# An encoder layer on one core: first-phase buffers, order and weight splits rearranged

## The chip, the cores and the metric

One core of a Trainium2 chip runs the whole layer in one launch. The metric is the device time of a launch in microseconds. The core has a tensor engine (PE), a vector engine (VectorE, DVE), a scalar engine (ScalarE, ACT) and a general one (GpSimd, POOL), each with its own instruction queue worked through in order, and DMA engines. SyncE (SP) issues nearly all transfers, ScalarE's queue some small ones.

## The reference

One post-norm layer on 512 tokens of width 1024, all in fp32:

```
h    = layer_norm(x)
proj = h @ w_in                      # 384 q latent | 256 kv latent | 32 rope key | 512 a | 512 g
attention, 8 heads: q = rms_norm(q latent) @ w_qb, k and v = rms_norm(kv latent) @ w_kvb,
                    rotary on 32 of 96 dimensions, softmax, p @ v
conv: a * sigmoid(g) -> depthwise convolution, width 31 -> layer_norm -> silu
h1   = layer_norm(2**0.25 * h + concat(attention, conv) @ w_o)
moe: router softmax, each of 16 experts takes its top 64 tokens,
     down(silu(x @ w_gate) * (x @ w_up)) * gate, added back
out  = layer_norm(2**0.25 * h1 + moe)
```

The expert weights are 16 x 3 matrices of 1024 x 2048 (or 2048 x 1024), some 400 MB; everything else is about 15 MB.

## The kernel before

The program has two phases. The first, up to line 998, does everything ahead of the experts; the second streams the expert weights through a ring of buffers and does each expert's three products (L1199, L1276). SBUF is cut into 20 numbered slots of 8 KB a partition, which serve one purpose after another: a slot that a stage has finished with takes the next weights, and finally the first expert weights (`stream`). So the end of a stage's use sets when later transfers can start.

Products of the first phase are made exact in parts. `split` (L226) copies a weight or activation rounded to fp32r on ScalarE ("hi") and subtracts it on another engine ("lo"); `mm3` (L256) then does three matmuls, hi x hi, hi x lo and lo x hi, at L258, L259 and L260. A projection of 128 columns (`project`) is 8 x 3 of them on 512 tokens.

The order on each engine is worked out by a planner that simulates the program: it takes operations by their place in the text when their inputs are ready in its model. `pin` (L206) keeps chosen operations of an engine in written order, for the engines in the set `ordered`. `filler` gives the convolution taps a place behind everything else.

The stages that the change touches, in order:

- `x` is normalised in four tiles (`xhat`, on ScalarE for even and VectorE for odd tiles), turned on PE (L392) and written as `hT`, hi on ScalarE (L393) and lo on VectorE (L395, L396), for 8 chunks. VectorE and GpSimd are pinned here, ScalarE isn't. The first two groups of w_in are split at the same time: four pieces ahead of the loop, the rest behind it.
- `w_in` comes in seven groups (`load_win`, L304), raw into slots 14 and 15 in turn, split into four pairs of slots (`split_win`).
- `conv_w` and `positions` are loaded by ScalarE's queue into buffers of `tmp()`, a rotation of four (L409 to L414); conv_w is turned by four transposes (L418).
- `glu(j)` projects a and g, does the tanh (L435), gates (L436), and then the 31 taps of the convolution: `n_act` of them on ScalarE (L444, L447), added on GpSimd (L445), the rest on VectorE (L453). It is called with 0, 0, 4 and 4.
- `keys`, `queries` and the values: `heads` projects into a PSUM bank and splits it (hi on ScalarE, lo on VectorE). PSUM has 3 banks of kind "pj", 2 "tr", 1 "st", 1 "cn", 1 "cv". For both pairs of heads in flight, rope keys and zeros are copied first (`copy_to`, L625, L627).
- attention in 16 units (`units`): scores two units ahead, softmax, turns (L757), p @ v (L772). `at(n)` puts side work behind unit n: loads of w_o at 9, splits of its first half at 11 and 13, loads of its second half at 13.
- `output(half, t, n)` multiplies by w_o: the attention half first, then the convolution half, whose norm has been done meanwhile.

## Time and profile before

| | us |
|---|---|
| three runs | 1202.52, 1203.52, 1205.8 |
| median | 1203.52 |
| the profiled execution | 1208.29 |
| its span | 1206.3 |

| engine | busy us | share of the span |
|---|---|---|
| PE, matmuls | 1119.5 | 93% |
| VectorE | 400.4 | 33% |
| ScalarE | 249.6 | 21% |
| GpSimd | 203.2 | 17% |

The span is one execution seen by the hardware profiler; the time around it is what the launch adds. Rows name an engine, the line of the kernel, the operation and `out<-in` by the program's names. An idle time in brackets is put down to the releaser that came last. A line can be that of a helper: L227 and L228 are every `split`. In the stretches each engine has its busy time and its count of instructions, and behind them stand PE's granted clock (1.00 is full), the DMA engines' mean share and GB/s.

### The profile page before, as it was taken

What the parts mean: (1) busy time and instruction counts of PE and PEld (TensorE: products, weight loads), DVE (VectorE), ACT (ScalarE), POOL (GpSimd) and SP (SyncE); (2) the same over time, 40 slices, a digit from 0 to 9 for tenths busy, and PEclk for the clock granted to TensorE, in tenths of its full rate; (3) what the DMA queues carried; (4) which work ended last, traced back from release to release, by engine and by line L of the source; (5) the groups of instructions that cost most, each with busy time, mean ns of one, the idle gap of its engine ahead of it and who ended that gap; (6) DMA issues with size and microseconds to landing.
All of it is one profiled execution on the core that took longest, in us unless ns stands there. A gap on an engine that the chain in (4) does not pass through costs nothing.

```text
span 1206.3 us, 13663 instructions
## 1 busy us (share of the span) xinstructions
PE 1119.5 (93%) x5573; PEld 545.0 (45%) x5573; DVE 400.4 (33%) x905; ACT 249.6 (21%) x448; POOL 203.2 (17%) x234
## 2 busy tenths in 40 slices
PE   5899998999999998999999999999998998899996
PEld 3687776785334343433343334334332433243432
DVE  6799898543011115122021112011210122011252
ACT  4546677321111111101010011001000101010120
POOL 6778467210000007000000000000000000000041
PEclk9899899999999999999999999999999999999999
DMA  6421014777999998999999999999999999999996
GB/s 200 135 84 36 6 71 144 271 268 281 420 429 428 428 393 343 427 430 427 426 427 428 428 426 430 427 426 429 426 428 429 426 428 426 429 426 427 428 427 253
DMA packets 43681, 422.85 MB, mean 351 GB/s; under 512 B 5178, under 2 KB 13187, under 8 KB 18018
## 3 DMA queue, kind: packets, MB, share of 16 engines
q1 hardware_dynamic: 42032, 421.28, 84.3%
q8 instruction: 44, 0.72, 0.2%
q10 hardware_dynamic: 1506, 0.43, 0.2%
q0 software_dynamic: 80, 0.26, 0.1%
q14 instruction: 19, 0.16, 0.0%
HBM read 419.60 MB, written 2.36 MB: 350 GB/s over the span
## 4 chain that ended last, share of the span: by engine, by line
PE 73%; DMA 16%; DVE 6%; ACT 2%; issue 1%; POOL 1%; POOLq 0%; SPq 0%; ACTq 0%; DVEq 0%
PE gu L1199 30%; PE py L1276 16%; DMA b<-in_w_up_dram 6%; PE sg L1044 5%; DMA b<-in_w_down_dram 4%; PE pj L258 4%; PE pj L259 3%; PE pj L260 3%; DMA b<-in_w_gate_dram 3%; PE sg L1091 3%; PE st L772 1%; DVE sq L1210 1%; PE tr L1066 1%; DVE cv L453 1%; DMA s<-in_w_in_dram 1%
## 5 line engine op out<-in xcount | busy, mean ns | idle before, releaser
L1199 PE MATMUL gu<-b,xg 128*64 128x512 f32 x1920 | 439.1, 598 | 22.1 <-DVE sq L1210 10.9
L1199 PEld LDWEIGHTS gu<-b,xg 128*64 128x64 f32 x1920 | 133.8, 137 | 291.1 <-issue 244.5
L1276 PE MATMUL py<-b,sq 128*64 128x512 f32 x976 | 224.1, 598 | 0.0
L1056 POOL COPY sq<-oh 128x256 f32<-128x256 f32 x16 | 5.9, 400 | 799.4 <-PE sg L1250 799.4
L1210 DVE TENSOR_TENSOR sq<-sq,gu 128x512 f32<-128x512 f32 x30 | 20.6, 687 | 292.6 <-PE gu L1199 276.8
L1276 PEld LDWEIGHTS py<-b,sq 128*64 128x64 f32 x976 | 67.3, 136 | 109.4 <-issue 102.2
L258 PE MATMUL pj<-s,s 128*128 128x512 f32 x189 | 78.4, 424 | 7.6 <-ACT q L435 3.2
L1044 PE MATMUL sg<-oh,h 128*128 128x128 f32 x512 | 72.6, 290 | 8.3 <-DVE oh L1035 6.9
L1045 ACT ACTIVATE xg<-sg,gbp 128x128 f32<-128x128 f32 x64 | 29.3, 457 | 237.6 <-PE sg L1044 145.9
L1044 PEld LDWEIGHTS sg<-oh,h 128*128 128x128 f32 x512 | 64.6, 198 | 29.6 <-issue 21.6
L259 PE MATMUL pj<-s,s 128*128 128x512 f32 x189 | 77.1, 408 | 0.0
L228 POOL TENSOR_TENSOR s<-s,s 128x512 fp32r<-128x512 f32 (+2 forms) x54 | 64.8, 1223 | 19.0 <-ACT s L227 12.2
L240 DVE SCALAR_TENSOR_TENSOR mask<-tr,aff,ones_b 128x128 bf16<-128x128 f32 x84 | 26.1, 348 | 120.7 <-PE tr L238 120.7
L260 PE MATMUL pj<-s,s 128*128 128x512 f32 x157 | 63.2, 406 | 0.0
L453 DVE SCALAR_TENSOR_TENSOR cv<-s,q,cv 128x512 f32<-128x512 f32 x83 | 62.2, 749 | 1.7
L1212 ACT ACTIVATE sq<-gu 128x1024 f32<-128x1024 f32 x16 | 16.4, 1024 | 217.9 <-PE gu L1199 217.9
L1095 DVE TENSOR_TENSOR b<-sg,b 128x512 f32<-128x512 f32 x56 | 37.0, 687 | 58.3 <-PE sg L1091 58.3
L1091 PE MATMUL sg<-q,q 128*128 128x512 f32 (+1 forms) x128 | 42.2, 437 | 7.0 <-DVE b L1095 5.9
L1080 ACT ACTIVATE q<-py,gates 64x512 fp32r<-64x512 f32 x30 | 20.5, 682 | 131.7 <-PE py L1276 119.0
L258 PEld LDWEIGHTS pj<-s,s 128*128 128x128 f32 x189 | 37.5, 200 | 16.8 <-ACT q L435 3.7
L1081 DVE SCALAR_TENSOR_TENSOR q<-py,gates,q 64x512 fp32r<-64x512 f32 x30 | 22.5, 748 | 65.2 <-ACT q L1080 65.0
L259 PEld LDWEIGHTS pj<-s,s 128*128 128x128 f32 x189 | 37.4, 198 | 7.1
(288 smaller groups left out, 1112.8 us busy)
## 6 DMA issues: line engine op xcount, KB each, us to landing
b<-in_w_down_dram SPq DMA_DIRECT2D x60, 2048.0 KB, 25.8
b<-in_w_gate_dram SPq DMA_DIRECT2D x60, 2048.0 KB, 27.5
b<-in_w_up_dram SPq DMA_DIRECT2D x60, 2048.0 KB, 28.0
s<-in_w_gate_dram SPq DMA_DIRECT2D x8, 1024.0 KB, 6.8
s<-in_w_in_dram SPq DMA_DIRECT2D x12, 512.0 KB, 5.2
s<-in_w_up_dram SPq DMA_DIRECT2D x6, 1024.0 KB, 7.1
s<-in_w_down_dram SPq DMA_DIRECT2D x6, 1024.0 KB, 11.6
s<-in_w_o_dram SPq DMA_DIRECT2D x4, 1024.0 KB, 7.1
```

The source lines that it names most:

```text
L228: pin(eng, eng.tensor_tensor(lo, src, hi.bitcast(F32), op=OP.subtract))
L258: tensor(nc.tensor.matmul(p, a[0], b[0], start=start, stop=False, **kw))
L259: tensor(nc.tensor.matmul(p, a[0], b[1], start=False, stop=False, **kw))
L260: tensor(nc.tensor.matmul(p, a[1], b[0], start=False, stop=stop, **kw))
L453: nc.vector.scalar_tensor_tensor(part if k < CW - 1 else cva[j], src[k], w[k], cva[j] if k == n_act else part, op0=OP.mult, op1=OP.add)
L1044: nc.tensor.matmul(here, rows, oh[:, t, :], start=t == 0, stop=t == TT - 1)
L1045: nc.scalar.activation(xg[:, cc, :], here, AF.Identity, scale=gbp[:, 0, cc:cc + 1], bias=gbp[:, 1, cc:cc + 1])
L1091: nc.tensor.matmul(pp[h], g[h][rs, ts], parts[h][k][rs, :], start=k == 0, stop=k == 1)
L1095: nc.vector.tensor_tensor(a, pp[h], a, op=OP.add)
L1199: nc.tensor.matmul(p[g * 64:(g + 1) * 64, b, :], xg[:, c, s * CAP:(s + 1) * CAP], ws[a][2 * b + g], start=c == 0, stop=c == DC - 1)
L1210: nc.vector.tensor_tensor(hh[:, x], sg[:, x], p[:, x], op=OP.mult)
L1276: nc.tensor.matmul(py[x * 64:(x + 1) * 64, :], hT2[:, b, j, g * 64:(g + 1) * 64], w[2 * a + hf], start=f == 0 and not last, stop=f == 15)
```

## The change

- `load_win` places groups 2 and 3 in slots 0 and 1 instead of 14 and 15.
- `idle` moves up, takes a kind of bank, and puts 30 matmuls of the identity, whose results nobody reads, ahead of everything on PE.
- ScalarE is pinned from `xhat(2)` on; one piece of a split stands ahead of the `hT` loop, the others one behind each chunk.
- `conv_w` and `positions` are loaded into quarters of slot 18 (`lat`), which the rope tables use later.
- `glu(0)` and `glu(1)` do three taps on ScalarE and GpSimd; `glu(3)` writes its tanh into `kraw[0]`. `load(5)` stands ahead of `glu(1)`.
- Rope keys and zeros of the second pair of heads are copied after the values; `keys(0)` and `queries(0)` use the "tr" banks.
- `split_wo` becomes a generator that goes column half by column half; two pieces are taken behind each of units 11 to 14, and the second half of w_o is loaded behind unit 15.

```diff
@@ -298,7 +298,7 @@
         def load_win(g):
             name, c0, n = WIN_GROUPS[g]
-            raw = slot(14 + g % 2)[:, :8 * n].rearrange("p (c n) -> p c n", c=8)
+            raw = slot((14, 15, 0, 1, 14, 15, 14)[g])[:, :8 * n].rearrange("p (c n) -> p c n", c=8)
             src = w_in[0, :, c0:c0 + n].rearrange("(c p) n -> p c n", p=128)
             raws[g] = raw
             return [lambda a=a: nc.sync.dma_start(raw[:, 4 * a:4 * a + 4], src[:, 4 * a:4 * a + 4]) for a in range(2)]
@@ -356,6 +356,14 @@
                 for _ in g:
                     pass
+        def idle(n, kind="pj"):
+            p = bank(kind)
+            for _ in range(n):
+                tensor(nc.tensor.matmul(p[:, :128], ident, ident, start=True, stop=True))
+        idle(30, "cv")
         hhi = quarters(slot(2, F32R)) + quarters(slot(3, F32R))
         hlo = quarters(slot(4, F32R)) + quarters(slot(5, F32R))
@@ -382,10 +390,10 @@
             vector(nc.vector.bn_aggr(mv[:, 0:2], st))
             pin(G, nc.gpsimd.tensor_scalar(mv[:, 2:3], mv[:, 1:2], LN_EPS, None, op0=OP.add))
             pin(G, nc.gpsimd.tensor_tensor(mv[:, 2:3], mv[:, 2:3], half_n, op=OP.pow))
+        ordered.add(nc.scalar)
         xhat(2)
         xhat(3)
-        for sp in (sp0, sp1, sp0, sp1):
-            next(sp)
+        next(sp0)
         for c in range(DC):
             p = bank("tr")
             for t in range(TT):
@@ -394,6 +402,8 @@
             hf = tmp()
             vector(nc.vector.tensor_scalar(hf, p, vc("eg", c), vc("eb", c), op0=OP.mult, op1=OP.add))
             vector(nc.vector.tensor_tensor(hlo[c], hf, hhi[c].bitcast(F32), op=OP.subtract))
+            next((sp1, sp0)[c % 2], None)
         run(sp0, sp1)
         ordered.clear()
@@ -406,11 +416,11 @@
         load_rows((("qg", q_norm_g, 3), ("kg", kv_norm_g, 2), ("cb", conv_b, 4), ("cg", conv_ln_g, 4),
                    ("cbb", conv_ln_b, 4)))
-        cwrow = tmp()[:CW]
+        cwrow = lat[2][:CW]
         nc.scalar.dma_start(cwrow, conv_w[0])
         rr = tp.tile([128, 2], F32, name="rr")
         nc.scalar.dma_start(rr, rope_rows)
-        pos_i = tmp().bitcast(I32)
+        pos_i = lat[3].bitcast(I32)
         nc.scalar.dma_start(pos_i, bcast(positions, S))
         to_columns(16, 33)
         pw = bank("cn")
@@ -427,11 +437,11 @@
             nc.gpsimd.memset(hp[j][:, 0:CW // 2], 0.0)
             nc.gpsimd.memset(hp[j][:, HP - CW // 2:HP], 0.0)
-        def glu(j, n_act=0):
+        def glu(j, n_act=0, sg=None):
             pa = project(QR + KVR + ROPE + j * 128)
             pg = project(QR + KVR + ROPE + CC + j * 128)
-            sg = tmp()
+            sg = tmp() if sg is None else sg
             nc.scalar.activation(sg, pg, AF.Tanh, scale=0.5)
             nc.vector.scalar_tensor_tensor(hp[j][:, CW // 2:CW // 2 + S], sg, 1.0, pa, op0=OP.add, op1=OP.mult)
             src = [hp[j][:, k:k + S] for k in range(CW)]
@@ -524,13 +534,13 @@
         load(2)
         load(3)
-        glu(0)
+        glu(0, 3)
         rope_tables()
         run(split_win(2))
         load(4)
-        glu(1)
+        load(5)
+        glu(1, 3)
         run(split_win(3))
-        load(5)
         s0, s1, s17 = slot(0, F32R), slot(1, F32R), slot(17, F32R)
         cqn = list(zip(quarters(s0)[:3], quarters(s1)[:3]))
         ckvn = list(zip((quarters(s0)[3], quarters(s1)[3]), quarters(s17)[:2]))
@@ -607,7 +617,7 @@
         rotary(0)
         rotary(1)
-        glu(3, 4)
+        glu(3, 4, kraw[0])
@@ -626,11 +636,14 @@
             else:
                 nc.scalar.activation(dst, src, AF.Identity)
-        for qe, ke, qo, ko in qk:
+        def same_rows(qe, ke, qo, ko):
             for k in range(2):
                 copy_to(k, ke[k][64:96], kpe[k][64:96].bitcast(F32), 64)
                 copy_to(k, ko[k][0:64], kpe[k][0:64].bitcast(F32), 0)
                 copy_to(0, qo[k][0:32], zero[:32].to_broadcast([32, S]), 0)
+        same_rows(*qk[0])
         def heads(i, w, n, src, even, odd, kind):
             p = bank(kind)
             for c in range(n):
@@ -649,14 +662,15 @@
                 for k in range(2):
                     copy_to(k, dst[k], qr[i // 2][32 * n:32 * n + 32, k, :].bitcast(F32), 32 * n)
-        keys(0, "pj")
-        queries(0, "pj")
+        keys(0, "tr")
+        queries(0, "tr")
         vt = quarters(slot(14))
         for i in range(4):
             p = bank()
             for c in range(2):
                 mm3(p, tuple(z[:, i * 128:(i + 1) * 128] for z in ckvn[c]), wv[c], c == 0, c == 1)
             nc.scalar.activation(vt[i], p, AF.Identity)
+        same_rows(*qk[1])
         wo, raw_wo = {}, {}
@@ -673,14 +687,17 @@
         def split_wo(half, q, raw, pair, engines):
             hi, lo = (slot(i, F32R).rearrange("p (c n) -> p c n", c=2) for i in pair)
-            for c in range(2):
-                for a in range(2):
+            for a in range(2):
+                for c in range(2):
                     cs = slice(a * 512, (a + 1) * 512)
                     split(hi[:, c, cs], lo[:, c, cs], raw[:, c, cs], engines[2 * c + a])
-            for c in range(2):
-                for n in range(2):
-                    i = (2 * q + c, n) if half == 0 else (4 + 2 * c + n, q)
-                    wo[i] = tuple(z[:, c, n * 512:(n + 1) * 512] for z in (hi, lo))
+                    i = (2 * q + c, a) if half == 0 else (4 + 2 * c + a, q)
+                    wo[i] = tuple(z[:, c, cs] for z in (hi, lo))
+                    yield
+        def pieces(n):
+            for i in range(n):
+                next(wo_split[i % 2], None)
         vrows.append(tp.tile([32, 128], F32, name="vrow0"))
@@ -818,13 +835,17 @@
                 split(cg_hi[j], cg_lo[j], sf, nc.gpsimd)
                 grp.append((cg_hi[j], cg_lo[j]))
+        wo_split = []
         def at(n):
             if n == 9:
                 raw_wo[0] = load_wo(0, 0, 15), load_wo(0, 1, 6)
-            if n == 11:
-                split_wo(0, 0, raw_wo[0][0], (12, 13), (G, G, V, G))
-            if n == 13:
-                split_wo(0, 1, raw_wo[0][1], (0, 1), (V, G, V, G))
+            if n == 10:
+                wo_split.extend((split_wo(0, 0, raw_wo[0][0], (12, 13), (G, G, V, G)),
+                                 split_wo(0, 1, raw_wo[0][1], (0, 1), (V, G, V, G))))
+            if 10 < n < 15:
+                pieces(2)
+            if n == 15:
                 raw_wo[1] = load_wo(1, 0, 6), load_wo(1, 1, 15)
             if 1 <= n < 9:
                 residual((n - 1) // 2, (n - 1) % 2)
@@ -877,9 +898,9 @@
         pm = conv_mean()
         for n in range(2):
             take(output(0, 2, n))
-        split_wo(1, 0, raw_wo[1][0], (2, 3), (G, G, V, V))
+        run(split_wo(1, 0, raw_wo[1][0], (2, 3), (G, G, V, V)))
         pvv = conv_norm(pm)
-        split_wo(1, 1, raw_wo[1][1], (4, 5), (G, G, G, V))
+        run(split_wo(1, 1, raw_wo[1][1], (4, 5), (G, G, G, V)))
         for n in range(2):
             take(output(0, 3, n))
         conv_out(pvv)
@@ -942,12 +963,6 @@
         def end_ranks(t):
             for e in range(2):
                 count(t, first_counts(e), masks.pop((t, e)))
-        def idle(n):
-            p = bank()
-            for _ in range(n):
-                tensor(nc.tensor.matmul(p[:, :128], ident, ident, start=True, stop=True))
         order = [(t, n) for n in range(2) for t in range(TT)]
         ordered.add(nc.tensor)
```

## Rows read from the trace of the kernel before

**Rows 1.** The page: busy us and share; DMA issues, KB each, us to landing

```profile
PE 1119.5 (93%) x5573; PEld 545.0 (45%) x5573; DVE 400.4 (33%) x905; ACT 249.6 (21%) x448; POOL 203.2 (17%) x234
...
s<-in_w_o_dram SPq DMA_DIRECT2D x4, 1024.0 KB, 7.1
```

**Rows 2.** Waits of PE, 0 to 290 us: total, times, longest, us

```profile
PE tr L392 <- ACT h L372: 7.7, 2, 4.1
PE cn L418 <- DMA q<-in_conv_w_dram: 3.9, 1, 3.9
PE pj L258 <- ACT q L435: 3.2, 2, 2.6
PE pj L258 <- DVE s L228: 2.5, 1, 2.5
```

**Rows 3.** Stretches of the first phase: length, busy us (instructions) per engine

```profile
31.94:46.33 14.39, 9.85 (x36) 7.72 (x36) 8.48 (x14) 4.69 (x9) 9.97 (x13) 0.76 0.57 172
46.33:113.54 67.21, 67.21 (x297) 55.25 (x297) 64.80 (x91) 34.91 (x63) 49.55 (x48) 1.00 0.21 65
113.54:130.75 17.21, 12.12 (x33) 9.32 (x34) 15.77 (x23) 9.50 (x17) 13.72 (x12) 0.70 0.11 31
130.75:180.00 49.25, 48.77 (x304) 36.73 (x303) 45.58 (x78) 37.79 (x81) 26.99 (x41) 1.00 0.12 43
180.00:195.50 15.50, 12.80 (x67) 7.88 (x65) 14.02 (x24) 11.81 (x26) 12.28 (x14) 0.89 0.38 134
```

**Rows 4.** The same view, ten-microsecond stretches of the expert phase

```profile
280.00:290.00 10.00, 10.00 (x57) 4.54 (x57) 1.53 (x10) 1.37 (x3) 0.00 (x0) 1.00 0.19 52
470.00:480.00 10.00, 10.00 (x46) 3.19 (x44) 5.70 (x4) 1.02 (x1) 7.89 (x6) 0.92 0.72 280
490.00:500.00 10.00, 10.00 (x56) 4.71 (x55) 1.05 (x3) 1.03 (x3) 0.00 (x0) 1.00 1.01 434
```

**Rows 5.** Chain that ended last, 0 to 130 us: start, us, what

```profile
29.69 6.10 DMA q<-in_conv_w_dram
38.90 0.43 PE pj L259
```

**Rows 6.** ScalarE in order of time, 11 to 33 us: start, us, [idle before]

```profile
11.67 0.63 ACT L227 ACTIVATE s<-s 128x512 fp32r<-128x512 f32 x1 [2.46 <-DMA s<-in_w_in_dram]
13.32 1.24 ACT L372 ACTIVATE h<-h,mve 128x1024 f32<-128x1024 f32 x1 [0.50 <-DMA s<-in_w_in_dram]
31.59 0.76 ACT L393 ACTIVATE s<-tr,q 128x512 fp32r<-128x512 f32 x1
```

**Rows 7.** Waits of SP's queue, 0 to 320 us

```profile
SPq L304 <- POOL s L228: 27.3, 8, 8.9
```

**Rows 8.** PE in order of time, one run of filler matmuls

```profile
271.71 1.95 PE L950 MATMUL pj<-ident 128*128 128x128 f32 x16
```

**Rows 9.** Groups by line, 0 to 290 us: busy, mean ns | idle before

```profile
L228 POOL TENSOR_TENSOR s<-s,s 128x512 fp32r<-128x512 f32 (+2 forms) x54 | 64.8, 1223 | 19.0 <-ACT s L227 12.2 <-PE pj L259 5.3 <-DMA q<-in_w_router_dram 1.5
...
L453 DVE SCALAR_TENSOR_TENSOR cv<-s,q,cv 128x512 f32<-128x512 f32 x83 | 62.2, 749 | 1.7
...
L445 POOL TENSOR_TENSOR s<-s,q 128x512 f32<-128x512 f32 x6 | 8.1, 1355 | 1.8 <-ACT q L444 1.8
```

**Rows 10.** VectorE in order of time, the last convolution tap

```profile
197.19 0.74 DVE L453 SCALAR_TENSOR_TENSOR s<-hp,q,cv 128x512 f32<-128x512 f32 x1
```

**Rows 11.** ScalarE in order of time, 114 to 116 us

```profile
114.43 1.13 ACT L627 ACTIVATE s<-s 64x512 fp32r<-64x512 f32 x2
115.47 0.57 ACT L435 ACTIVATE q<-pj 128x512 f32<-128x512 f32 x1
```

**Rows 12.** ScalarE in order of time, at 181 us

```profile
181.74 1.15 ACT L227 ACTIVATE s<-s 128x512 fp32r<-128x512 f32 x2 [1.09 <-DMA s<-in_w_o_dram]
```

**Rows 13.** SP's queue in order of time, the second w_o half

```profile
188.55 2.38 SPq L670 DMA_DIRECT2D s<-in_w_o_dram  x2
```

**Rows 14.** PE in order of time, first use of the conv group's low part

```profile
236.51 0.39 PE L260 MATMUL pj<-s,sq 128*128 128x512 f32 x1
```

## The prediction

> **What bounds the kernel now.** The page comes first: TensorE is busy for 93% of the span [rows 1], so the time can fall only where TensorE idles or runs at its lower clock. Next, the waits of PE up to 290 us (the first phase) show where it idles: 3.9 us in front of the four conv_w transposes, 2.6 us behind a tanh (L435), 2.5 us behind a subtraction on VectorE (L228), and a stall of 4.1 us before any projection [rows 2]. The stretches of that phase add the clock, the third number from the end of a row (one level is 2.4 GHz, 1.00, the other 1.2): 0.76, 0.70 and 0.89 in the three stretches with those stalls and a later one, 1.00 in the two between, where PE is busy nearly all the time [rows 3]. So I read each bad stretch as useful work (busy time times granted clock) and loss. From 31.94 to 46.33 us that is 9.85 x 0.76 = 7.5 us of work in 14.4, a loss of 6.9. From 113.54 to 130.75 it is 12.12 x 0.70 = 8.5 in 17.2, a loss of 8.7. From 180 to 195.5 it is 12.80 x 0.89 = 11.4 in 15.5, a loss of 4.1 [rows 3]. Together 19.7 us.
>
> Does a gain there reach the end? In the expert phase DMA moves 434 GB/s at 490 us, but 52 GB/s at 280 us and 280 GB/s at 470 us while PE is busy all through both stretches [rows 4]: up to 480 us the weight stream waits for PE to free buffers, and after it the stream sets the pace. Both start from PE's progress, so what PE gains before 280 us I carry to the end one for one.
>
> **The change part by part.**
>
> *conv_w and positions into `lat`.* The transposes of conv_w stand in PE's queue before further projection matmuls. Their transfer is issued only at 29.69 us, when a `tmp()` buffer is free, and takes 6.10 us [rows 5]. In `lat[2]`, unused until the rope tables, it can be issued in the first microseconds. The stall of 3.9 us goes and so does the half clock behind it, where a matmul takes 0.43 us [rows 5] against 67.21 / 297 = 0.23 [rows 3]. Of the 6.9 us I leave about 0.6 for the tanh wait at the stretch's end (L435 has 3.2 us in two waits, the longest 2.6 [rows 2]): 6.3 us. Bounds 0 and 6.9. What is late next there is hT: the last ScalarE writes of it come at 31.59 us and after, behind splits of later w_in groups [rows 6]; the next edit is for that.
>
> *ScalarE pinned, splits interleaved.* At present ScalarE waits 2.46 us for w_in, does a split at 11.67 and reaches the third normalised tile only at 13.32 [rows 6]. In written order that tile goes first: 0 to 13.32 - 11.67 = 1.65 us earlier. The fourth tile, on VectorE, must come too, so I take half, 0.8 us. Eight splits between eight hT writes cost nothing that PE sees: ScalarE is busy 4.7 of 14.4 us there [rows 3]. GpSimd's subtractions keep the same order with them.
>
> *w_in groups 2 and 3 into slots 0 and 1, load(5) earlier.* SP's queue waits 27.3 us in eight waits for splits to free slots 14 and 15 [rows 7]. Four transfers no longer do, and conv_w travels on ScalarE's queue, not behind them. PE has no wait on w_in in [rows 2], so this is worth nothing by itself; it keeps the later groups from being late when the projections start earlier, and without it part of those 27.3 us would come to stand on PE's path.
>
> *30 filler matmuls at the start.* Sixteen such take 1.95 us [rows 8], so 30 take about 3.7, or 7.3 at half clock, while PE has nothing else. Worth 0 to 2.4 us: the upper end is the half-clock part of the conv_w loss, 6.9 - 3.9 - 0.6. I take 0, since stalls of up to 4.1 us lie between the fillers and the first projection [rows 2], and stalls of 2.6 and 2.5 us were enough to leave a stretch at 0.70 [rows 2, 3]. The Trainium skill ("TensorE: Matmul & The Clock Gate", section "What's actually happening") says that the slow state is the default and activity releases it; by that rule alone the fillers would pay, and the sum below would be 2.4 us larger.
>
> *Six taps of glu(0) and glu(1) from VectorE to ScalarE and GpSimd.* VectorE loses 6 x 749 ns = 4.5 us; ScalarE gains six, being busy 34.91 of 67.21 us [rows 3], GpSimd four additions of 1.36; VectorE's price and GpSimd's are in [rows 9]. Nobody on PE's path waits for a tap now, but VectorE has little room: 64.80 + 15.77 + 45.58 + 14.02 = 140.2 us busy of the 149.2 from 46.33 to 195.5 [rows 3], and the last tap runs at 197.19 [rows 10]. With 4.5 less it has 135.7 us to do. So the stages behind it can shrink by up to 13.5 us before VectorE is full, and the taps are what makes room for the next two terms. Their own value: 0.
>
> *Own tanh buffer in glu(3), "tr" banks for keys(0) and queries(0), the second pair's copies later.* Before the tanh at 115.47 ScalarE runs copies that nobody needs yet (two of them from 114.43 [rows 11]); PE waits for the bank that the tanh reads, then for a bank that keys(0) holds until VectorE's subtraction. In "tr" banks keys and queries need neither, and the four value products come behind them. Work of 8.5 us took 17.2; bounds 0 and 8.7. I take 6, two thirds, since the scores still need VectorE's four subtractions of keys and queries, queued among taps of 0.75 us.
>
> *w_o split in pieces.* ScalarE waits 1.09 us for a w_o transfer at 181.74 and does splits in a row [rows 12], with the exponentials that PE needs behind them. Two pieces per step in place of four shorten the burst, but a piece can still sit in front of an exponential until its transfer has landed. Bounds 0 and 4.1; I take half, 2.0. The second w_o half is loaded two steps later. Now it is issued at 188.55 [rows 13], lands in 7.1 [rows 1], and the convolution group is first used at 236.51 [rows 14]: over 40 us of cover, so 10 us later cost nothing; without that cover each microsecond would count.
>
> Sum: 6.3 + 0.8 + 6 + 2.0 = 15.1, taken as 15. The profiled execution took 1208.29 us, 2.0 beyond its span of 1206.3, and would come to 1193.3. The median shown, 1203.52, lies 4.8 below it; there the forecast is 1188.5 us. The bounds of the terms are 0 and 6.9 + 1.65 + 2.4 + 8.7 + 4.1 = 23.8, so 1179.7 to 1203.5.
>
> **Rivals.**
>
> *VectorE takes over.* If it keeps its 9.0 us of idle time, the attention side can shrink only by the 4.5 us of taps: 6.3 + 0.8 + 4.5 = 11.6. If each of the four GpSimd additions also holds it up for its 1.36 us, 6.2 remain. Middle 9, so 1194.5 us. For it: 64.80 of 67.21 us busy [rows 3]. Against it: in the stalls VectorE ran taps, which is work done early and not lost. Chance 0.20 (gains of 4 to 11 us).
>
> *All terms at their upper ends,* the first projections at full clock included: around 22 us, 1181.5. For it: nothing in the views shows another releaser right behind the removed ones. Chance 0.14 (gains over 19).
>
> *The stalls only move.* The order on each engine is planned anew from modelled times; conv_w's transposes may again stand before a late transfer, or hT be late in their place (31.59 [rows 6]). Then only some 2 us come: 1201.5. Chance 0.10.
>
> *Slower: the new taps block the tanh buffers.* Each new tap holds a rotating `tmp()` until GpSimd has added it, and GpSimd is busy 9.97 of 14.39 us with splits just then [rows 3]. If the additions stand behind three groups of splits, 12 x 1.22 us = 14.6 (64.8 us in 54 of them over the phase [rows 9]), the next tanh waits, and the projection banks with it. PE can do one projection meanwhile, 24 x 0.23 = 5.5, and comes back at half clock, 2.4: 11.5 per tanh, 23.0 for the two, against the 15: 1211.5 us. It decides from nine splits ahead of an addition (7.9 per tanh); with fewer the stalls stay under the gain. Against it: glu's additions are written before the splits of groups 2 and 3. Chance 0.09.
>
> **How the numbers follow.** The forecast, gains of 11 to 19 us, has 0.47. A difference under 0.3%, 3.6 us, can't be told from none. Faster: 0.47 + 0.20 + 0.14 = 0.81; same 0.10; slower 0.09. The range leaves out the slower case and the best tip of the third: 1179.5 to 1203. The likeliest case's own range is 1184.5 to 1192.5.
>
> **What would show it.** After the change: the conv_w transfer issued before 15 us and no PE wait at its transposes; PE busy and at clock 1.00 from about 20 us through the first four projections; no wait of over 1 us at glu(3), keys(0) and queries(0), and the scores starting within some 11 us of the last rotary matmul; the clock at 0.95 or more in the w_o stretch; the last tap about 15 us earlier; the first expert matmul 15 us earlier, and the end with it. The prediction is wrong if the first expert matmul comes 15 us earlier and the end doesn't, if VectorE's last tap moves by less than PE's work around it, or if the first projections already start at full clock.

## The result, and the profile after

The changed kernel takes 1221.88 us (median of 4 runs, 1221.48 to 1222.68) beside 1204.66 for the kernel before on the same chip (four runs now, with the three of the table above): ratio 1.0144, 95% interval 1.0126 to 1.0161. That is 17 us slower where 15 us faster was forecast, and outside the range. The profiled execution took 1222.68 us with a span of 1220.8.

First the page of the changed kernel, its line of engines in the columns of [rows 1].

```profile
PE 1134.9 (93%) x5633; PEld 556.8 (46%) x5633; DVE 404.6 (33%) x899; ACT 254.2 (21%) x454; POOL 211.5 (17%) x238
```

PE's share hasn't moved. Its waits, 0 to 310 us, are other ones than in [rows 2]: one tanh (L445 is the old L435), two subtractions on VectorE, the first hT write, and still conv_w.

```profile
PE pj L258 <- ACT q L445: 5.6, 1, 5.6
PE pj L259 <- DVE s L228: 4.7, 1, 4.7
PE pj L258 <- ACT s L401: 4.3, 1, 4.3
PE cn L428 <- DMA s<-in_conv_w_dram: 3.6, 1, 3.6
PE pj L260 <- DVE s L228: 2.7, 1, 2.7
```

The stretches, cut at the first projection, the first, second and fourth tanh, the first transposed probabilities, the first p_v and the start of the last row of p_v matmuls (columns of [rows 3]):

```profile
22.01:43.40 21.39, 20.66 (x86) 15.81 (x86) 15.80 (x18) 14.24 (x31) 20.85 (x20) 0.86 0.14 32
43.40:64.80 21.40, 15.11 (x58) 11.96 (x58) 14.30 (x11) 10.64 (x15) 18.55 (x14) 0.86 0.51 148
64.80:125.20 60.40, 59.73 (x258) 49.24 (x259) 54.75 (x80) 31.90 (x62) 44.88 (x44) 0.97 0.16 54
125.20:142.80 17.60, 11.70 (x41) 7.84 (x40) 17.44 (x23) 9.79 (x20) 13.71 (x15) 0.84 0.09 31
142.80:154.90 12.10, 12.10 (x56) 10.53 (x54) 11.34 (x23) 6.95 (x16) 2.84 (x7) 0.67 0.00 1
154.90:229.80 74.90, 71.30 (x430) 50.27 (x431) 65.64 (x108) 55.22 (x114) 48.42 (x59) 0.98 0.29 100
```

The clock is below 1.00 in all of them; before, the two long stretches of [rows 3], 67 and 49 us, were at 1.00. The start times of the same work in every kernel of this study place the loss (us from the span's start, read from the engines in order of time; "last p_v" is the last of its 128 matmuls, "held" the longest VectorE operation between 112 and 135 us):

```
                    ratio   first hT  4th tanh  1st exp  1st p_v  last p_v  1st expert  held
before              1        16.5     115.5     133.2    142.3    217.3     280.4       3.21
changed             1.0144   21.2     125.2     140.4    154.9    231.1     294.1       5.46
- w_in slots back   1.0152   17.7     122.4     137.7    152.8    228.8     293.0       5.34
- no taps           1.0087   20.9     118.3     132.3    148.3    226.1     290.2       3.48
- both              1.0121   17.2     115.8     130.9    145.6    221.5     289.4       5.31
- no fillers        1.0125   21.7     125.7     141.0    155.4    231.7     294.6       5.47
- first stage only  1.0173   20.9     124.9     138.4    147.4    221.6     296.8       1.35
before + attn + w_o 1.0096   17.0     115.5     129.3    144.3    223.1     286.8       3.42
before + attn       1.0079   16.8     114.5     128.3    143.3    222.1     285.8       3.43
before + tanh buf.  1.0036   16.6     115.3     133.3    143.4    219.9     283.0       3.20
before + banks      1.0059   17.7     116.3     133.0    147.1    220.7     283.7       4.25
before + copies     0.9996   16.6     114.1     130.3    139.5    213.9     277.0       3.20
before + w_o        0.9982   16.5     113.9     129.0    137.9    214.2     278.4       3.20
before + lat        1.0037   18.5     115.5     135.6    143.6    222.3     285.5       5.73
```

Of the 13.7 us by which the experts start later, 9.7 are there at the fourth tanh and 12.6 at the first p_v. The last tap now runs at 210.06, not 197.19 [rows 10].

At the start, ScalarE in order of time ("ACTq" are the transfers it issues):

```profile
8.09 0.23 ACTq L420 DMA_DIRECT2D s<-in_conv_w_dram  x1
...
19.69 0.31 ACTq L291 DMA_DIRECT2D vrow<-in_ln_b_dram  x1
20.73 0.40 ACTq L718 DMA_DIRECT2D q<-in_w_router_dram  x1
21.18 0.78 ACT L401 ACTIVATE s<-tr,q 128x512 fp32r<-128x512 f32 x1 [8.16 <-DMA vrow<-in_ln_b_dram]
```

conv_w is issued early as forecast, but PE still waits for it, and its transposes run only at 17.35; ScalarE's small transfers, issued between 9.90 and 12.87 us before, now come up to 20.73, ahead of the first hT write in the same queue. From 10 to 20 us DMA moves 326 GB/s (130 before): the first eight w_in transfers are all issued by 17.8 us, without waiting for a slot. (Later ones wait: SP's queue stands 32.9 us in six waits for splits, 27.3 in eight before [rows 7].) hT starts 4.6 us later.

Then the tanh of 64.81, VectorE in order of time; L478 is the old L468, four operations on two operands in SBUF, 990 ns each before:

```profile
51.11 1.49 DVE L475 TENSOR_SCALAR q<-q 128x512 f32<-128x512 f32 x1 [4.92 <-POOL s L455]
52.63 1.40 DVE L476 TENSOR_SCALAR q<-q 128x512 f32<-128x512 f32 x1
54.07 6.75 DVE L478 SCALAR_TENSOR_TENSOR q<-q,q 128x512 f32<-128x512 f32 x4
```

and GpSimd beside it, where the new taps' additions (L455) stand among splits:

```profile
43.40 6.43 POOL L228 TENSOR_TENSOR s<-s,s 128x512 fp32r<-128x512 f32 x5
49.77 1.31 POOL L455 TENSOR_TENSOR s<-s,q 128x512 f32<-128x512 f32 x1
51.02 5.86 POOL L228 TENSOR_TENSOR s<-s,s 128x512 fp32r<-128x512 f32 x4
56.84 1.74 POOL L455 TENSOR_TENSOR s<-s,q 128x512 f32<-128x512 f32 x1
```

The rope table waits for the first addition, then runs slowly beside the splits. ScalarE has the sine next and only behind it the tanh (62.26 and 64.81): PE's 5.6 us.

### The profile page after: what moved, and what is told of

Same layout as the page of the kernel before. It is cut to its first block, busy times and chain, and to the rows that moved or that the text cites. A ratio compares the mean times of both kernels' runs of the same rounds, so it can differ in the third digit from the quotient of the medians.

```text
span 1220.8 us, 13773 instructions
## 1 busy us (share of the span) xinstructions
PE 1134.9 (93%) x5633; PEld 556.8 (46%) x5633; DVE 404.6 (33%) x899; ACT 254.2 (21%) x454; POOL 211.5 (17%) x238
## 4 chain that ended last, share of the span: by engine, by line
PE 69%; DMA 15%; DVE 6%; POOL 5%; issue 3%; ACT 2%; POOLq 0%; DVEq 0%; ACTq 0%; SPq 0%
PE gu L1214 29%; PE py L1291 17%; DMA b<-in_w_up_dram 9%; PE sg L1059 5%; DMA b<-in_w_down_dram 4%; PE pj L258 3%; PE pj L260 3%; PE pj L259 3%; PE sg L1106 2%; POOL s L228 2%; PE tr L1081 1%; DVE sq L1225 1%; DMA out_dram<-h 1%; PE st L789 1%; POOL s L635 1%
## 5 line engine op out<-in xcount | busy, mean ns | idle before, releaser
L258 PE MATMUL pj<-s,s 128*128 128x512 f32 x184 | 74.9, 415 | 11.8 <-ACT q L445 5.6
L259 PE MATMUL pj<-s,s 128*128 128x512 f32 x184 | 74.4, 404 | 0.4 <-DVE s L404 0.4
L260 PE MATMUL pj<-s,s 128*128 128x512 f32 x152 | 60.8, 403 | 1.6 <-POOL s L228 1.6
L463 DVE SCALAR_TENSOR_TENSOR cv<-s,q,cv 128x512 f32<-128x512 f32 x77 | 57.8, 750 | 1.7
L258 PEld LDWEIGHTS pj<-s,s 128*128 128x128 f32 x184 | 35.8, 194 | 20.7 <-ACT q L445 6.1
L1096 DVE SCALAR_TENSOR_TENSOR q<-py,gates,q 64x512 fp32r<-64x512 f32 x30 | 22.5, 749 | 56.5 <-ACT q L1095 56.2
L259 PEld LDWEIGHTS pj<-s,s 128*128 128x128 f32 x184 | 35.8, 195 | 8.0 <-DVE s L404 1.3
```

The source lines that it names most:

```text
L258: tensor(nc.tensor.matmul(p, a[0], b[0], start=start, stop=False, **kw))
L259: tensor(nc.tensor.matmul(p, a[0], b[1], start=False, stop=False, **kw))
L260: tensor(nc.tensor.matmul(p, a[1], b[0], start=False, stop=stop, **kw))
L463: nc.vector.scalar_tensor_tensor(part if k < CW - 1 else cva[j], src[k], w[k], cva[j] if k == n_act else part, op0=OP.mult, op1=OP.add)
```

## The experiments

**The first stage: w_in slots, taps, both undone.**

```diff
-            raw = slot((14, 15, 0, 1, 14, 15, 14)[g])...
+            raw = slot(14 + g % 2)...
-        glu(0, 3)   ...   glu(1, 3)
+        glu(0)      ...   glu(1)
```

> The changed kernel with w_in groups 2 and 3 back in slots 14 and 15. Theory 1 (ScalarE's queue: its small transfers wait for completions that the four early w_in transfers hold up, so the first hT write comes at 21.2 us instead of 16.5): the first hT write comes before 17 us, the first projection about 5 us earlier, and the time falls by 5 to 10 us, to 1212 to 1217. Theory 2 (the new taps hold the rotating buffers, the rope tables and with them the second tanh come late): the tanh wait of 5.6 us stays and the time stays within 3 us of 1222. Pinning as the cause: no change at the start either, since ScalarE's written order is the same.

> The changed kernel with no taps of glu(0) and glu(1) on ScalarE. Theory 2: PE's wait for the second tanh (5.6 us, and half clock behind it) goes, the time falls by some 7 us to 1215; the late start of 21.2 us stays. Theory 1 alone: within 2 us of 1222, and VectorE's 4.5 us of extra taps might even add some.

> Both of the above undone. If theories 1 and 2 are separate and add, 1207 to 1210 us, with the late start and the tanh wait both gone and the wait at the first scores (4.7 us) left; if one of them hides the other, no faster than the better of the two alone.

Measured: 1.0152 (1.0119 to 1.0186), 1.0087 (1.0059 to 1.0115) and 1.0121 (1.0095 to 1.0147). 1.0152 is not the fall of 5 to 10 us that theory 1 named, and 1.0121 not the 1207 to 1210 us of two theories that add. In both kernels with the slots back, `load(5)`, which the change had moved ahead of group 3's splits, fills slot 15 before they read it: they leave group 3's weights out and split group 5's in their place. So these two measure the slots together with a transfer that waits for less, and the slots' figures below are to be read with that. In the table the four kernels form a square: at the fourth tanh the taps cost 6.9 us (125.2 to 118.3) or 6.6 (122.4 to 115.8), the slots 2.8 or 2.5; without both it stands at 115.8, as before. So the taps and the slots are the whole loss up to there, and the other first-stage edits together bring nothing. At the end the square does not close as well: with the slots moved the taps cost 6.9 us (1.0144 - 1.0087), with the slots back 3.7 (1.0152 - 1.0121). The slots' 2.5 us does not show in the time; without the taps it is 4.1 us longer with the slots back, by intervals that overlap.

**The 30 fillers left out** (the line `idle(30, "cv")`).

> The changed kernel without the 30 filler matmuls at the start. They are 60 passes, 10.1 us of PE from 1.4 us on, and hold the first transposes to 11.48 us, 2.2 later than before. Theory G (they only delay the start): 1 to 2.5 us faster than the changed kernel. Theory H (they keep the clock for the first projections): 1 to 3 us slower. If the first hT write at 21 us is set by the small transfers in ScalarE's queue alone: within 0.7 us of the changed kernel (1221.9), which the prediction's term of 0 says too.

1.0125 (1.009 to 1.0159): no difference from the changed kernel that can be told, so the term of 0 stands. Its size did not: the fillers are 60 records and fill 10.1 us.

```profile
1.42 6.97 PE L363 MATMUL cv<-ident 128*128 128x128 f32 x34 [1.42 <-DVE ident L167]
...
8.48 3.17 PE L363 MATMUL cv<-ident 128*128 128x128 f32 x26
```

**The attention side and the w_o pieces on the kernel before, together and alone** (the hunks of the diff from `glu(3, 4, kraw[0])` to `same_rows(*qk[1])`, and those of `split_wo` and `at`).

> The kernel before with only the attention side of the change: own tanh buffer in glu(3), tr banks for keys(0) and queries(0), the second pair's copies later, w_o in pieces. The prediction's terms say 8 us faster than before (6 and 2), 1196. Theory 3 (the wait only moves to the first scores, behind a long VectorE operation beside a row of GpSimd's): within 3 us of 1204, with a PE wait of several us at the first scores.

> The kernel before with the attention side alone: glu(3)'s tanh in its own buffer, keys(0) and queries(0) in "tr" banks, the second pair's copies behind the value products; w_o as before. Both parts together were 10.3 us slower than the kernel before in one profile and comparison. Theory A (the attention side starts the scores earlier, but VectorE then owes its taps to the stages behind, and the first p_v comes later): this part alone is 5 to 8 us slower, first exponential near 129, first p_v near 144. Theory B (the w_o pieces cost it: splits in front of exponentials): this part alone is 2 to 8 us faster, first p_v before 142. The prediction on record: 6 us faster.

> The kernel before with the w_o splits in pieces of two per step and the second half loaded at step 15, nothing else. Theory A (the attention side is what costs): within 3 us of the kernel before, last p_v within 2 us of 215.9. Theory B (w_o pieces cost): 5 to 9 us slower, with ScalarE in a row of split pieces ahead of exponentials and PE's clock under 1.00 from 190 to 210 us. The prediction on record: 2 us faster.

1.0096 (1.0071 to 1.0122), 1.0079 (1.0052 to 1.0105), 0.9982 (0.9964 to 1.0001). The attention side alone costs 9.5 us; the pieces bring 2.2 us, not surely more than none. With the attention side PE is busy 5.00 of 5 us from 110 to 115 and 4.81 to 120, so the waits for the tanh at 113 us and for a subtraction of keys at 122 are gone. In their place PE idles among the first scores, 2.3 us from 121.5 and 1.8 from 124.5 (all PE waits over 1 us, 115 to 160 us):

```profile
PE pj L258 <- ACT s L661: 2.5, 2, 2.3
PE pj L260 <- DVE s L228: 1.8, 1, 1.8
PE tr L760 <- ACT s L766: 1.3, 1, 1.3
```

and the scores then run at half clock:

```profile
120.00:125.00 5.00, 2.21 (x9) 1.16 (x7) 4.91 (x6) 3.23 (x6) 5.00 (x5) 1.00 0.08 21
125.00:130.00 5.00, 3.21 (x8) 2.17 (x9) 4.91 (x10) 1.27 (x3) 2.07 (x5) 0.57 0.01 2
130.00:135.00 5.00, 5.00 (x24) 4.53 (x22) 4.93 (x10) 2.70 (x7) 1.58 (x3) 0.50 0.01 3
135.00:140.00 5.00, 5.00 (x19) 4.03 (x18) 4.93 (x10) 0.75 (x2) 0.19 (x1) 0.56 0.00 0
```

VectorE's column reads 4.91 to 4.93 of 5 throughout. The first exponential comes 4.9 us earlier, the first p_v 1.0 later: 15.0 us lie between them, 9.1 before.

**The attention side in three.** The tanh buffer, the banks, the copies, each alone on the kernel before.

> The kernel before with one part of the attention side: glu(3)'s tanh in kraw[0]. The whole side was 8 to 9 us slower, all of it after the fourth tanh: its stall of 2.55 us in front of keys(0) went, PE then idled 4.3 us between 121 and 126 us, and ran at half clock to 139. Theory A (the stall only moves behind the value products, and which order the scores get decides): this part alone is within 3 us, the wait for the tanh at 113.5 us gone or short, the first p_v between 140 and 144. Theory E (each part pulls the scores ahead of VectorE's maxima): 2 to 5 us slower. The prediction on record put 6 us of gain on the whole side.

> The kernel before with one part of the attention side: keys(0) and queries(0) in "tr" banks. Theory A (the banks let the value products run ahead and put the whole idle time, 4 to 5 us in one piece, just in front of the scores, with half clock behind it to the first p_v): 5 to 9 us slower, half clock from 126 to 139 us, 14 to 16 us from the first exponential to the first p_v (9.1 before). Theory F (the copies' place is what costs): within 2 us.

> The kernel before with one part of the attention side: the second pair's copies written behind the value products. Theory F (copies now stand among value evictions on ScalarE and make PE wait at them, as L661 did for 2.3 us): 4 to 8 us slower. Theory A (banks cost): within 2 us, since these copies have no reader before the second pair's scores.

1.0036 (1.0020 to 1.0053), 1.0059 (1.0041 to 1.0077), 0.9996 (0.9973 to 1.0019). The banks cost 7.1 us: three waits of 6.5 us together stand at the first scores, and from 125 to 140 us PE is busy 9.70 of 15 us at 0.58. The longest of them, 3.3 us, ends at a VectorE subtraction that stood behind a copy:

```profile
124.14 4.25 DVE L689 COPY gb<-q 128x32 f32<-128x32 f32 x1
128.42 0.69 DVE L228 TENSOR_TENSOR s<-tr,s 64x512 fp32r<-64x512 f32 x1
```

This copy of SBUF to SBUF takes 0.23 us in the kernel before. So the 7.1 us are not the banks' order alone, and how much of them is the copy was not measured.

The tanh buffer costs 4.3 us by itself; its wait stayed (2.6 us), so the tanh was not held up by `tmp()`. Why its first p_v is 1.1 us late and its last 2.6 is open. The copies are free.

**conv_w and positions in `lat` alone, and the first stage without the rest.**

```diff
-        cwrow = tmp()[:CW]
+        cwrow = lat[2][:CW]
-        pos_i = tmp().bitcast(I32)
+        pos_i = lat[3].bitcast(I32)
```

> The kernel before with conv_w and positions in lat[2] and lat[3], nothing else: the conv_w transfer can start in the first microseconds. Theory C (the stall at the conv_w transposes is worth what the stretch lost): 5 to 7 us faster, no PE wait at these transposes, the first four tanhs near 40, 49, 91 and 110 us and the first exponential near 127. Theory D (GpSimd's and VectorE's work paces that stretch and the gain is given back before the scores): under 2.5 us faster, first exponential within 2 us of 133.2.

> The changed kernel with the attention side and the w_o pieces put back as before: the first stage's edits alone (lat, w_in slots, the pinned start, fillers, taps). If the losses add up (whole change +17, attention side and w_o +10): 5 to 8 us slower than the kernel before, the first exponential near 140. If the late start and the taps are the whole loss whatever follows: 14 us slower or more. If the attention side only costs because of what stands ahead of it: within 3 us.

`lat` alone: 1.0037 (1.0022 to 1.0051). PE's wait at the conv_w transposes is gone and the first tanh comes at 42.5 (45.7), yet the second stands at 54.5 (54.7), the fourth at 115.5 as before, and the scores come later. On ScalarE the second tanh stands behind the sine, and the sine waits for the rope table on VectorE. Two of the table's operations on two operands in SBUF, with `lat` and then in the kernel before:

```profile
43.19 3.37 DVE L468 SCALAR_TENSOR_TENSOR q<-q,q 128x512 f32<-128x512 f32 x2
```

```profile
43.42 1.42 DVE L468 SCALAR_TENSOR_TENSOR q<-q,q 128x512 f32<-128x512 f32 x2
```

From 40 to 45 us GpSimd is busy 5.00 of 5 us with `lat` and 0.93 before: the stall at conv_w had emptied it. The last of the table's operations ahead of the sine starts at 50.6 and 50.7, so the gain is gone. Then, ahead of the scores, VectorE in order of time:

```profile
116.84 0.65 DVE L703 TENSOR_TENSOR q<-q,gb 128x128 f32<-128x128 f32 x1
117.41 0.74 DVE L453 SCALAR_TENSOR_TENSOR cv<-s,q,cv 128x512 f32<-128x512 f32 x1
118.06 0.67 DVE L436 SCALAR_TENSOR_TENSOR hp<-q,pj 128x512 f32<-128x512 f32 x1
118.66 5.73 DVE L703 TENSOR_TENSOR q<-q,gb 128x128 f32<-128x128 f32 x1
124.31 0.67 DVE L228 TENSOR_TENSOR s<-pj,s 64x512 fp32r<-64x512 f32 x1
```

and GpSimd in the same microseconds:

```profile
118.52 2.03 POOL L625 TENSOR_TENSOR s<-q,zero 64x512 fp32r<-64x512 f32 x2
120.52 1.28 POOL L726 TENSOR_TENSOR h<-h,s 128x512 f32<-128x512 f32 x1
121.75 1.26 POOL L228 TENSOR_TENSOR sq<-q,sq 128x512 fp32r<-128x512 f32 x1
122.98 1.25 POOL L445 TENSOR_TENSOR s<-s,q 128x512 f32<-128x512 f32 x1
124.20 1.30 POOL L726 TENSOR_TENSOR h<-h,s 128x512 f32<-128x512 f32 x1
```

The same operation takes 0.65 us and then 5.73, as long as five GpSimd operations in a row, and the subtractions for keys and queries stand behind it. `lat` is not at fault, as the next experiments show; it shifted the two engines against each other. The first stage alone: 1.0173 (1.0138 to 1.0208), worse than the whole change. It has no held operation and the table's shortest way from the fourth tanh to the first p_v (22.5 us). It loses 12 us behind the last p_v, where its new order puts the convolution's output behind output blocks: ScalarE waits 15.5 us for it, and PE stands 3.8 and 3.0 us at splits. The parts don't simply add.

**The held operations taken off VectorE.**

```diff
-            nc.vector.tensor_tensor(wr2[:, :, a], wr2[:, :, 1], gb...
+            nc.gpsimd.tensor_tensor(wr2[:, :, a], wr2[:, :, 1], gb...
```

alone in the first two, in the other two with the last addition of `rope` on GpSimd and the copy into `gb` on ScalarE.

> conv_w and positions in lat, as in the run that was 4.5 us slower, and the two multiplications of the router's rows by the gain (q<-q,gb, 128x128) on GpSimd in place of VectorE. In that run one of the two, which reads two operands from SBUF, took 5.73 us at 118.66 beside an unbroken run of GpSimd operations (the other 0.65), and VectorE's subtractions for keys(0) and queries(0) stood behind it. Theory L (held-up VectorE operations in front of the scores are the cost): no VectorE operation over 2 us between 116 and 130 us, the first p_v by 140 us (143.6 with lat alone), 3 to 5 us faster than lat alone, so 1.003 falls to 1.000 or under. Theory D (VectorE's and GpSimd's load alone paces the stretch): within 1.5 us of lat alone, since these two take 1.2 us of VectorE when free.

> The changed kernel with the same two multiplications on GpSimd; there one took 5.46 us at 130.42. Theory L: no VectorE operation over 2 us between 126 and 142, the first p_v 3 to 5 us earlier (154.9), about 4 us faster than the changed kernel: 1218. Theory A (tr banks and order alone put PE's idle time in front of the scores): within 1.5 us of it, and half clock from 138 to 150 us stays.

> The kernel before with the attention side (9.5 us slower alone), and three VectorE steps that read SBUF alone taken off VectorE: the two multiplications and the last addition of rope (q<-q,q) on GpSimd, the copy of the gains (gb<-q) on ScalarE. With the attention side alone the addition took 3.43 us at 118.38. Theory L: no VectorE operation over 2 us from 112 to 130, PE's idle time between 120 and 127 us 2 to 4 us less, half clock to 139 us shortened, 3 to 6 us faster than the attention side alone (1216): 1210 to 1213. Theory A: 1215 to 1217. If GpSimd's load (1.3 us more for each addition) delays the splits instead: over 1217.

> A version meant to beat both: the kernel before with the w_o pieces alone (2.2 us faster) and the three steps off VectorE. There the addition took 3.20 us at 117.94 and PE waited 2.52 us for VectorE's subtraction behind it. Theory L: that wait under 1 us, the first p_v by 136 us (137.9), 1 to 3 us faster than the pieces alone: 1201 to 1204. If GpSimd's load takes its place: 1205 to 1208.

`lat`: 0.9986 (0.9973 to 1.0000) in place of 1.0037, 6 us for moving two small operations; first p_v 138.2, as theory L has it. From 107 us to the held operation the two kernels run the same VectorE operations, save the first of the moved two, in the same order, at most 0.4 us apart; where the other was held, the subtraction follows at once (118.55 us, 124.31 with `lat` alone). The PE waits from 60 to 145 us, first with `lat` alone, then without the held operation:

```profile
PE pj L258 <- ACT q L435: 4.7, 1, 4.7
PE pj L258 <- ACT s L659: 3.7, 1, 3.7
```

```profile
PE pj L258 <- ACT q L435: 4.7, 1, 4.7
PE pj L258 <- ACT s L659: 0.7, 2, 0.6
```

The attention side: 1.0028 (1.0015 to 1.0040) in place of 1.0079, 6 us too, but not where theory L put it: the first p_v stays late (143.9), and the gain lies behind it (last p_v 217.9, not 222.1). Three steps give VectorE more room than the held one alone, so this run does not tell holding from load; the one with `lat` does, since the two multiplications take 0.6 us together where GpSimd is idle (0.29 and 0.28 with the banks alone) and 1.2 in the kernel before. The changed kernel: 1.0118 (1.0100 to 1.0137), not surely less than 1.0144; its first p_v comes 2.6 us earlier and its last at the same time, half clock stays, so there theory A holds. With the w_o pieces: 1.0005 (0.9993 to 1.0017), no gain, though PE's wait for VectorE's subtraction (2.5 us) was gone; 1.4 us came back at another VectorE operation.

**The maxima's product on VectorE,** on top of the third of these (L747, `m * rq`, 128x1).

> The attention side with the three steps off VectorE, as in the run that was 3.4 us slower than the kernel before, and the product of each row maximum with the query scale (L747, 0.18 us on GpSimd) on VectorE. In that run the first maximum was reduced at 122.30, its product ran at 126.10 behind GpSimd's splits and additions, the first exponential at 126.31, and PE waited 4.3 us and then ran at half clock to 139. Theory P (GpSimd's queue in front of the exponentials is the rest of the loss): first exponential by 124, no PE wait over 2 us between 120 and 130, the first p_v by 138 (143.9), 3 to 6 us faster than that run: 1204 to 1207. Theory A (banks and order put the idle time there whatever the products do): within 1.5 us of that run, 1209 to 1212.

1.0137 (1.0107 to 1.0168): 13 us slower than without this edit, the opposite of theory P. VectorE in order of time:

```profile
125.14 7.84 DVE L747 TENSOR_TENSOR mx<-mx,rq 128x1 f32<-128x1 f32 x1
...
138.83 0.15 DVE L747 TENSOR_TENSOR mx<-mx,rq 128x1 f32<-128x1 f32 x1
```

GpSimd in the same time, and then PE's wait for the exponential behind it:

```profile
125.26 2.47 POOL L729 TENSOR_TENSOR h<-h,s 128x512 f32<-128x512 f32 x2
127.69 1.25 POOL L228 TENSOR_TENSOR sq<-q,sq 128x512 fp32r<-128x512 f32 x1
128.91 1.25 POOL L445 TENSOR_TENSOR s<-s,q 128x512 f32<-128x512 f32 x1
130.13 0.39 POOL L706 TENSOR_TENSOR q<-q,gb 128x128 f32<-128x128 f32 x1
130.49 2.47 POOL L729 TENSOR_TENSOR h<-h,s 128x512 f32<-128x512 f32 x2
```

```profile
PE pj L258 <- ACT s L749: 10.6, 1, 10.6
```

An operation of 0.15 us on one column took 7.84 us while these seven GpSimd operations went by. PE's wait behind it is 10.6 us, and it ran at half clock from there to 150 us. What GpSimd's queue ahead of the exponentials costs was not learnt from this run.

**A version meant to beat both:** `lat`, the two multiplications on GpSimd, and the w_o pieces.

> A version meant to beat both: the kernel before with conv_w and positions in lat, the two router multiplications on GpSimd, and the w_o pieces, without the attention side, the taps, the fillers and the w_in slots. If the two gains add up (1.7 us and 2.2 us by their ratios): 1201 to 1203 beside 1205.7, ratio 0.997 with an interval below 1. If both gains were the same one (no held-up VectorE operation and full clock in front of the scores): 1203.5 to 1204.5. If the plan moves another two-operand operation into GpSimd's run: over 1206, with a VectorE operation over 3 us between 112 and 130.

0.9994 (0.9981 to 1.0007): the two small gains don't add. No kernel here beats the one before by more than 0.2%.

## Why the prediction was wrong

- *conv_w stall, 6.3 us.* The step held where it was read: without the stall the first tanh comes 3.2 us earlier. What failed is that this reaches the scores. By 115 us nothing of it is left, and the time is 4.5 us longer. In the changed kernel the wait itself only moved: 3.6 us, at 13.7 instead of 31.9 us. I set VectorE's idle time against rows of busy time and argued that work done in a stall is not lost; but a VectorE operation has no fixed duration here, and the one held for 5.73 us was worth 6 us of time. The 3.2 us are gone by the second tanh already, in the same way: the rope table's VectorE operations slow down beside GpSimd.
- *Attention side, 6 us.* The largest error: 9.5 us slower alone. PE's stalls went as forecast, in front of keys(0). But PE then reached the scores before their operands, idled there twice within 5 us, and ran at half clock nearly to the first p_v. The rival "VectorE takes over" names the engine; it charged no clock behind the new wait, and so could not come out slower. 6 of the 9.5 us come back when VectorE's SBUF steps are taken away; the other 3.4 were not settled, and the one guess that was tried (GpSimd's queue ahead of the exponentials) could not be told, because its test ran into a held operation.
- *Six taps, 0.* Measured 6.9 us, by the ratios of the changed kernel and the one without them (3.7 by the other pair). The mechanism is the one of the slower rival: the additions stand behind splits on GpSimd and hold buffers. The victim was the rope table on VectorE, with the tanh behind its sine, not a tanh's buffer directly; it happened once, not twice. Its ground against, that glu's additions are written first, did not hold in the planned order.
- *w_in slots, 0.* They make the first hT late by 3 to 4 us (21.2 against 17.7, 20.9 against 17.2): their transfers start at once, and ScalarE's small ones come late. I had counted SP's waits [rows 7] and not ScalarE's issues. It did not show in the time.
- *ScalarE pin, 0.8.* Not tried alone; with `lat`, interleaved splits and fillers it is worth nothing at the fourth tanh.
- *Fillers, 0.* Right by the time, with their length wrong: 16 records in [rows 8] are the eight matmuls of `idle(8)`, so 30 matmuls were 60 records, and the 3.7 us were 10.1.
- *w_o pieces, 2.0.* Measured 2.2, interval -0.1 to 4.3. The number agrees by luck, as far as the traces show: PE is busy 7.8 of 10 us from 180 to 190 us, before and with the pieces, at a granted clock of 0.92 and 0.66; the lead is 4.4 us at the first p_v, ahead of any w_o split, and only 2.0 at the first expert matmul. Some 3 us of it are the clock's (last section).
- *One for one to the end.* Right: 13.7 us at the first expert matmul, 14.5 at the span's end.

The costs that I put beside the terms are 4.5 + 9.5 - 2.2 + 6.9 = 18.7 us, beside 17.2 for the whole. That they come near is no proof that they add: the first stage alone cost 20.9 us, the attention side with the pieces 11.6, and together that is nearly twice the whole. Shown by experiment are the taps up to the fourth tanh, the attention side's loss, and the held operation with `lat`; how the losses share the 17 us stays open.

## What to carry to other kernels

A stall in front of one engine may be the slack of another: before removing it, look at which engine is full in the stretch behind it, and at how its operations' durations spread, not at their mean. Where VectorE and GpSimd are both full, look for VectorE operations whose operands all lie in SBUF and that PE's operands stand behind; one small step on the wrong engine was worth 6 us one way and 13 the other. Taking them off VectorE paid in two kernels of four (with `lat` and with the attention side), so it is to be tried, not assumed. To let such an operation read one operand from PSUM is a second way that the durations below suggest and no run tried.

## What the runs showed of the hardware that was not expected

A VectorE operation with its operands in SBUF can be held for many GpSimd operations in a row: 128x128 at 0.28 us with GpSimd idle, 0.65 or 5.73 beside it, 128x1 at 0.15 or 7.84, a copy of 128x32 at 0.23 or 4.25; taps and subtractions that read one operand from PSUM kept their 0.75 and 0.68 us beside the same GpSimd runs. The Trainium skill ("SBUF — State Buffer", section "SBUF: two separate sides") says that VectorE with two SBUF inputs and GpSimd share a port pair, which the first to start keeps for its whole instruction. The traces agree that one waits. What they add is that VectorE, held, waited for the running GpSimd instruction and four or seven more. What lets it in at last is open. The profile counts the hold as busy time, so no view of waits shows it.

The clock does not answer equal stalls equally. In the kernel before and in that with the w_o pieces, PE runs the same instructions through two stalls of 2.5 us; after the second, the one restarts at half clock and stays there for 14 matmuls, some 3 us, the other at full clock (0.50 and 1.00 from 125 to 130 us). First the kernel before, then the other:

```profile
124.26 0.77 PE L258 MATMUL pj<-s,s 128*128 128x512 f32 x1 [2.54 <-DVE s L228]
```

```profile
122.68 0.47 PE L258 MATMUL pj<-s,s 128*128 128x512 f32 x1 [2.52 <-DVE s L228]
```

So 3 us of one profiled execution can be the clock's draw, which is as much as several of the terms of this sum. The executions of the kernel before spread the same way: 11 with a mean granted clock of 0.995 took 1202.7 to 1203.7 us, 20 with 0.988 took 1206.4 to 1211.1.
